# Moving the differences of the down weights from VectorE in a down projection to GpSimd in the mixers, with GpSimd's own loads and stores

## The chip, the cores and the metric

The kernel runs on one core of one Trainium2 chip. The metric is the time on the device in microseconds, from one launch. Engines are named as the profile names them: PE is TensorE (matmul), with PEld its weight loads; DVE is VectorE; ACT is ScalarE; POOL is GpSimd; SP is SyncE, which here only issues transfers. Each engine takes its instructions in order, its DMA issues among them. On-chip memory is SBUF, and PE writes to PSUM.

## The reference, cut to what matters

One layer of a hybrid encoder runs on a prompt of 2048 rows and on 128 sample rows, all of width 1024 in float32:

```python
h = rms_norm(x, norm_g[0])
z = h @ w_in                      # q, k, v of attention; q, k, v, o and two gates of the mLSTM
att = band_attention(qa, ka, va)  # chunks of 64, own chunk + 8 before, learned relative bias
hb = mlstm_sequence(qh, kh, vh, ig, lf, ...)
mix = concat(rms_norm(att), sigmoid(ob) * head_norm(hb)) @ w_out
x = x + rms_norm(mix, norm_g[1])
u = rms_norm(x, norm_g[2]) @ w_up                 # 1024 -> 2 x 2816
y = causal_depthwise_conv(u, width=3)
gate, up = split(y)
x = x + rms_norm((gelu(gate) * up) @ w_down, norm_g[3])     # w_down: 2816 x 1024
```

Matmuls are made accurate by splitting each operand into a high part `h` and a rest `l`, and three matmuls `hh + hl + lh` per product (`mm3`, L102 to L106).

## The kernel before, in words

**Mixers.** The prompt is worked in two halves of 8 tiles of 128 rows; the sample tile goes with the first. In each half, 14 groups of 256 columns of `w_in` are projected one after the other (`va0`, `qk0`, `qk1`, `va1`, `qk2`, `qk3`, then `qb` and `vo` in turn). A loop (L1245) walks the groups; each group is a generator that yields after every 12 matmuls. After each yield, `pump` (L183) lets two further streams go on, attention and mLSTM, by a balance of estimated PE and DVE times. PE makes `qk` in PSUM, ACT copies it out as `qk_st` (L236, L238) and issues its store to `qTd` or `kTd`; SP loads it again as `qraw` and `kraw`, and ACT and DVE split these into `qs`, `kh`, `kl`. `wi_h` and `wi_l` are the split weights of the next group. At the start `relrow` is built in device memory (the bias, one row per query), and its parts `nb` are loaded and edged on POOL (L338, L339). POOL also masks `mb` of the mLSTM (L685), makes the small roots `mf` from `ad` (L658, L659), and completes the keys `skr` of the sample attention (L860).

**Feed-forward.** The 17 tiles go in three blocks. Each block runs an up projection (22 steps), then a down projection. Blocks 1 and 2 multiply by a fast 2 x 2 scheme with 7 products in place of 8, which needs differences of the four blocks of 512 columns `B11, B12, B22, B21` in which `w_down` is laid out (11 rows of four blocks). Block 0's down projection takes the plain weights, 22 steps for each half of the columns (`dh` 0 and 1). Beside it, one row of four blocks in every four steps is loaded, turned into differences on DVE and stored in device memory as `wtd`, from where `down_rows` (L1363) loads it in blocks 1 and 2 under the name `wdr`. `gr` and `gh`, `gl` are the activations, `fr` the copy of a finished PSUM tile (L1394), `h2T_pt`, `b` and `t` the transposed input of the next block's up projection. At the switch from `dh` 0 to 1 six tiles are copied to `fr` by DVE, and PE's next matmuls write where they lay.

**Order.** The program text gives an order, and a scheduler places instructions on each engine by its own estimate of times. Instructions wrapped in `keep_in_program_order` keep their order among each other. Tiles come from pools with a fixed number of buffers; the four tiles of a row come from `spare`:

```python
spare = ctx.enter_context(tc.tile_pool(name="spare", bufs=6, reuse_waits="tile"))    # L56

for k in ks:                                   # down projection, block 0
    ...
    for j in order if k == NF - 1 else range(nt):
        down(j, k, wh, wl)
    if k >= 1:
        ahead.step()
    if b == 0:
        next(fold, None)                       # L1866
```

A row's third and fourth tile therefore wait until stores of the row before have landed. `store_a` (L1576) makes the matching differences of the activations in blocks 1 and 2 on DVE.

## Time and profile before

| | us |
|---|---|
| three runs, median (lowest to highest) | 2769.21 (2767.95 to 2771.8) |
| the profiled execution | 2768.76 |
| its span, first to last instruction | 2767.0 |
| PE, DVE, ACT, POOL busy | 2693.8, 1943.2, 1438.5, 654.3 |

Stretches by name: the first projections begin at 12 us, the mixers and `w_out` end near 1316 us, block 0's up projection runs to 1638 us, its down projection to 1840 us, and blocks 1 and 2 follow.

How to read it: a group row shows line, engine, operation, output and inputs, shape, count, then busy us, mean ns of one, and the idle us before with what ended them. A row in order of time starts with its start and duration in us; in brackets stands how long the engine was idle before, and what released it. A row of waits has us in total, times, longest. A matmul's end is modelled, so successive matmuls overlap in such rows. A row on an issue (`ACTq`, `SPq`, `POOLq`) has KB and the median us from issue to landing.

### The profile page before, as it was taken

What the parts mean: (1) busy time and instruction counts of PE and PEld (TensorE: products, weight loads), DVE (VectorE), ACT (ScalarE), POOL (GpSimd) and SP (SyncE); (2) the same over time, 40 slices, a digit from 0 to 9 for tenths busy, and PEclk for the clock granted to TensorE, in tenths of its full rate; (3) what the DMA queues carried; (4) which work ended last, traced back from release to release, by engine and by line L of the source; (5) the groups of instructions that cost most, each with busy time, mean ns of one, the idle gap of its engine ahead of it and who ended that gap; (6) DMA issues with size and microseconds to landing.
All of it is one profiled execution on the core that took longest, in us unless ns stands there. A gap on an engine that the chain in (4) does not pass through costs nothing.

```text
span 2767.0 us, 47747 instructions
## 1 busy us (share of the span) xinstructions
PE 2693.8 (97%) x16422; PEld 2520.4 (91%) x16422; DVE 1943.2 (70%) x3615; ACT 1438.5 (52%) x2918; POOL 654.3 (24%) x1271
## 2 busy tenths in 40 slices
PE   8999999999999999999999999999999999999998
PEld 7899999998899998878999998789999878999976
DVE  5344455646546668766989987668888876998956
ACT  4355555645356666543545455445455665554554
POOL 1000010211100002344434322123332212455401
PEclk9999999999999999999999999999999999999999
DMA  5534355556554456355645559866785777787775
GB/s 184 158 116 139 105 161 173 158 155 210 166 180 143 140 168 195 108 167 196 229 153 187 168 189 326 300 222 205 230 239 174 248 235 231 222 257 230 247 261 178
DMA packets 326017, 536.11 MB, mean 194 GB/s; under 512 B 60002, under 2 KB 159806, under 8 KB 325646
## 3 DMA queue, kind: packets, MB, share of 16 engines
q1 hardware_dynamic: 248382, 393.82, 45.7%
q0 software_dynamic: 32464, 93.87, 10.4%
q10 hardware_dynamic: 44928, 45.37, 5.1%
q8 instruction: 129, 2.11, 0.3%
q14 instruction: 114, 0.93, 0.1%
HBM read 383.28 MB, written 159.08 MB: 196 GB/s over the span
## 4 chain that ended last, share of the span: by engine, by line
PE 53%; DVE 3%; DMA 2%; issue 1%; POOL 1%; ACT 1%; DVEq 0%; POOLq 0%; SPq 0%; ACTq 0%
PE uec L104 6%; PE uec L105 6%; PE uec L106 6%; PE dn L106 4%; PE dn L105 4%; PE dn L104 4%; PE ua L106 3%; PE ua L105 3%; PE ua L104 3%; PE wo L106 2%; PE wo L104 2%; PE wo L105 2%; PE dnm L106 2%; PE dnm L105 2%; PE dnm L104 2%
## 5 line engine op out<-in xcount | busy, mean ns | idle before, releaser
L104 PE MATMUL uec<-B,wuh 128*128 128x384 f32 (+1 forms) x720 | 236.1, 328 | 4.1 <-DVE uu L1644 4.1
L105 PE MATMUL uec<-B,wuh 128*128 128x384 f32 (+1 forms) x720 | 235.3, 327 | 0.0
L106 PE MATMUL uec<-B,wul 128*128 128x384 f32 (+1 forms) x720 | 234.1, 327 | 0.0
L1309 ACT CAST wuh<-wu 128x512 fp32r<-128x512 f32 x255 | 141.7, 618 | 108.8 <-PE uec L105 100.9
L1310 DVE TENSOR_TENSOR wul<-wu,wuh 128x512 fp32r<-128x512 f32 x255 | 165.5, 685 | 4.0 <-DMA x2d<-mx 2.8
L405 DVE CUSTOM_DVE_ANT_0 tmp<-s,nb 128x640 f32<-128x640 f32 (+4 forms) x128 | 94.4, 737 | 95.1 <-PE s L395 93.5
L104 PE MATMUL vo<-wi_h,hT 128*128 128x256 f32 x544 | 155.1, 285 | 0.6 <-DVE mt L211 0.6
L106 PE MATMUL vo<-wi_h,hT 128*128 128x256 f32 x544 | 155.6, 286 | 0.0
L105 PE MATMUL vo<-wi_l,hT 128*128 128x256 f32 x544 | 154.8, 285 | 0.0
L104 PEld LDWEIGHTS uec<-B,wuh 128*128 128x128 f32 x720 | 135.2, 188 | 6.6 <-DVE uu L1644 5.5
L104 PE MATMUL qk<-hT,wi_h 128*128 128x384 f32 (+1 forms) x384 | 128.5, 335 | 7.3 <-ACT qk_st L236 5.9
L105 PEld LDWEIGHTS uec<-B,wuh 128*128 128x128 f32 x720 | 135.4, 188 | 0.3
L106 PEld LDWEIGHTS uec<-B,wul 128*128 128x128 f32 x720 | 135.1, 188 | 0.0
L418 DVE TENSOR_TENSOR ptl<-pt,pth 128x640 fp32r<-128x640 f32 (+4 forms) x128 | 93.6, 737 | 55.9 <-ACT pth L417 54.8
L406 ACT ACTIVATE tmp<-tmp,mn 128x640 f32<-128x640 f32 (+4 forms) x128 | 97.6, 762 | 67.0 <-DVE mn L405 62.9
L1310 DVE TENSOR_TENSOR wdl<-wdr,wdh 128x512 fp32r<-128x512 f32 x198 | 125.1, 685 | 7.3 <-ACT wdh L1309 7.0
L1310 DVE TENSOR_TENSOR al<-ar,ah 128x768 fp32r<-128x768 f32 (+2 forms) x94 | 70.9, 764 | 82.5 <-ACT ah L1309 81.0
L105 PE MATMUL qb<-hT,wi_h 128*128 128x384 f32 (+1 forms) x384 | 127.9, 333 | 0.0
L105 PE MATMUL qk<-hT,wi_h 128*128 128x384 f32 (+1 forms) x384 | 127.5, 332 | 0.0
L106 PE MATMUL qk<-hT,wi_l 128*128 128x384 f32 (+1 forms) x384 | 127.2, 331 | 0.0
L106 PE MATMUL qb<-hT,wi_l 128*128 128x384 f32 (+1 forms) x384 | 127.2, 331 | 0.0
L104 PE MATMUL qb<-hT,wi_h 128*128 128x384 f32 (+1 forms) x384 | 127.1, 331 | 0.0
(445 smaller groups left out, 9373.0 us busy)
## 6 DMA issues: line engine op xcount, KB each, us to landing
wu<-in_w_up SPq DMA_DIRECT2D x220, 256.0 KB, 4.9
wu<-wsd SPq DMA_DIRECT2D x176, 256.0 KB, 4.8
wdr<-in_w_down SPq DMA_DIRECT2D x110, 256.0 KB, 5.0
wi_raw<-in_w_in SPq DMA_DIRECT2D x52, 512.0 KB, 4.0
wsd<-ws POOLq DMA_DIRECT2D x88, 256.0 KB, 3.6
wdr<-wtd SPq DMA_DIRECT2D x88, 256.0 KB, 5.3
gr<-gd SPq DMA_DIRECT2D x39, 384.0 KB, 6.0
kraw<-kTd SPq DMA_DIRECT2D x112, 128.0 KB, 3.2
```

Of the source, the lines that this page charges most:

```text
L104: nc.tensor.matmul(out, ah, bh, start=start, stop=False, skip_group_check=onto)
L105: nc.tensor.matmul(out, ah, bl, start=False, stop=False, skip_group_check=onto)
L106: nc.tensor.matmul(out, al, bh, start=False, stop=stop, skip_group_check=onto)
L405: nc.vector.tensor_tensor_reduce(o_, s_, b_, 1.0, 3e38, ALU.add, ALU.min, accum_out=mn)
L406: nc.scalar.activation(tmp[:, :n], tmp[:, :n], AF.Exp, bias=mn, scale=-1.0, accum_out=rsum[:, i % 4, hh:hh + 1])
L418: nc.vector.tensor_tensor(s.ptl[:, sl, qc], ptv, s.pth[:, sl, qc], op=ALU.subtract)
L1309: nc.scalar.copy(h, r)
L1310: nc.vector.tensor_tensor(l, r, h, op=ALU.subtract)
```

## The change: what it does

The generator of the differences is started before the mixers and advanced once after each yield of the first half's projection groups, from group 1 (`qk0`) on, until its 99 steps are through, and no longer in block 0's down projection. Loads, subtractions and stores are all on POOL; before, they were on ACT's queue, DVE and POOL's queue. Loads and stores stay of 256 KB, and the number of each stays 44. The third difference is formed with the other sign, so the fourth is a sum, and `store_a` gives the matching activation difference the other sign too.

```diff
+FOLD_AT = 1
...
-    def folds(period, plan):
+    def folds():
+        keep = tc.keep_in_program_order
         live = {}
 
         def load(k, xs):
             if k < NK:
                 for x in xs:
                     live[k, x] = spare_tile(f"fold{k}_{x}")
-                    tc.keep_in_program_order(nc.scalar.dma_start(live[k, x], I["w_down"][k][:, x * 512:(x + 1) * 512]))
+                    keep(nc.gpsimd.dma_start(live[k, x], I["w_down"][k][:, x * 512:(x + 1) * 512]))
 
-        def combine(k):
+        def store(k, xs):
+            for x in xs:
+                keep(nc.gpsimd.dma_start(wtd[k][:, x * 512:(x + 1) * 512], live.pop((k, x))))
+
+        for k in range(NK):
+            load(k, (0, 1))
+            yield
+            load(k, (2, 3))
+            yield
+            yield
+            yield
             a, b, c, d = [live[k, x] for x in range(4)]
-            for o, x, y in ((a, b, a), (b, c, b), (c, c, a), (d, d, c)):
-                tc.keep_in_program_order(nc.vector.tensor_tensor(o, x, y, op=ALU.subtract))
-
-        def store(k):
-            if k >= 0:
-                for x in range(4):
-                    tc.keep_in_program_order(nc.gpsimd.dma_start(wtd[k][:, x * 512:(x + 1) * 512], live.pop((k, x))))
-        ...
+            for o, x, y, op in ((a, b, a, ALU.subtract), (b, c, b, ALU.subtract), (c, a, c, ALU.subtract),
+                                (d, d, c, ALU.add)):
+                keep(nc.gpsimd.tensor_tensor(o, x, y, op=op))
                 yield
-        if live:
-            store(NK - 1)
+            store(k, range(4))
+            yield
...
             pump(pe + sum(a[0] for a in ahead), dve + sum(a[1] for a in ahead))
+            if half == 0 and gi >= FOLD_AT:
+                next(fold, None)
...
-    fold = folds(4, {0: ("ab",), 1: ("cd",), 3: ("combine", "store")})
...
-            for o, x, y in ((s3, a11, a21), (s2, a22, s3), (s4, a12, s2)):
-                nc.vector.tensor_tensor(o, x, y, op=ALU.subtract)
+            for o, x, y, op in ((s3, a11, a21, ALU.subtract), (s2, s3, a22, ALU.subtract), (s4, a12, s2, ALU.add)):
+                nc.vector.tensor_tensor(o, x, y, op=op)
...
-                    if b == 0:
-                        next(fold, None)
```

Three places of the new order. POOL, early in the mixers, before: after the last norm of the first half it has only the edging of `nb` and the masks `mb`, in this row.

```order
L338 MEMSET nb_0_1243 64x64
L339 MEMSET nb_0_1243 64x64
L338 MEMSET nb_0_1314 64x64
L339 MEMSET nb_0_1314 64x64
L685 AFFINE_SELECT mb_0_4002<-mb_0_4002 128x256
L685 AFFINE_SELECT mb_2_4103<-mb_2_4103 128x256
```

POOL at the same place, now. The whole first row of blocks (loads, four operations, stores) and the second's loads stand ahead of this piece; `fold_0` to `fold_3` are the four blocks of a row.

```order
L1194 TENSOR_TENSOR fold_0_1110<-fold_1_1112,fold_0_1110 128x512
L1194 TENSOR_TENSOR fold_1_1112<-fold_2_1147,fold_1_1112 128x512
L1194 TENSOR_TENSOR fold_2_1147<-fold_0_1110,fold_2_1147 128x512
L1194 TENSOR_TENSOR fold_3_1149<-fold_3_1149,fold_2_1147 128x512
L339 MEMSET nb_0_1271 64x64
L340 MEMSET nb_0_1271 64x64
L1182 DMA wtd_244<-fold_0_1110 128x512
L1182 DMA wtd_244<-fold_1_1112 128x512
L1182 DMA wtd_244<-fold_2_1147 128x512
L1182 DMA wtd_244<-fold_3_1149 128x512
L1178 DMA fold_0_1313<-in_w_down 128x512
L1178 DMA fold_1_1315<-in_w_down 128x512
```

The small operations now stand between pieces of the work on the differences, and before the first `mb` three rows of blocks are done and the fourth is half loaded. Later on, the last two rows of blocks stand so among `skr` and `ad`:

```order
L861 COPY skr_0_3873<-own_3871 128x16
L1194 TENSOR_TENSOR fold_0_3780<-fold_1_3782,fold_0_3780 128x512
L861 COPY skr_1_3893<-own_3871 128x16
L861 COPY skr_2_3917<-own_3871 128x16
L1194 TENSOR_TENSOR fold_1_3782<-fold_2_3802,fold_1_3782 128x512
L1194 TENSOR_TENSOR fold_2_3802<-fold_0_3780,fold_2_3802 128x512
L861 COPY skr_3_3948<-own_3871 128x16
L1194 TENSOR_TENSOR fold_3_3804<-fold_3_3804,fold_2_3802 128x512
```

Behind this piece come four stores, four loads and one more subtraction, and only then `ad` and `mf`; before, the four `skr` and `ad` followed each other directly.

ACT at the first attention head, in the second group's projections, before (`kTd` and the like are stores, `qk` is PSUM):

```order
L236 COPY qk_0_st_0_1052<-qk_0_1_0_984 128x384
L251 DMA kTd_0_81<-qk_0_st_0_1052 128x384
L354 CAST qs_0_1274<-qraw_0_1247 128x512
L236 COPY qk_0_st_1_1094<-qk_0_1_1_1055 128x384
L251 DMA kTd_0_81<-qk_0_st_1_1094 128x128
L251 DMA kTd_1_82<-qk_0_st_1_1094 128x256
```

And now:

```order
L237 COPY qk_0_st_0_1064<-qk_0_1_0_994 128x384
L252 DMA kTd_0_81<-qk_0_st_0_1064 128x384
L237 COPY qk_0_st_1_1114<-qk_0_1_1_1067 128x384
L252 DMA kTd_0_81<-qk_0_st_1_1114 128x128
L252 DMA kTd_1_82<-qk_0_st_1_1114 128x256
L355 CAST qs_0_1306<-qraw_0_1275 128x512
```

The cast `qs`, which needs the load `qraw`, has moved behind one more copy out of `qk`. On PE, the matmuls of attention move back by some tens of projection matmuls in the same stretch, and from the place where the last difference is stored the two orders of PE are alike.

DVE at the switch of block 0's down projection, before:

```order
L1394 COPY fr_0_20510<-dn_0_1_19636 128x512
L1310 TENSOR_TENSOR gl_1_1_20573<-gr_1_1_20464,gh_1_1_20572 128x768
L1181 TENSOR_TENSOR fold_0_20456<-fold_1_20458,fold_0_20456 128x512
L1310 TENSOR_TENSOR wdl_1_20531<-wdr_1_0_20532,wdh_1_20530 128x512
L1181 TENSOR_TENSOR fold_1_20458<-fold_2_20488,fold_1_20458 128x512
L1310 TENSOR_TENSOR wdl_1_20531<-wdr_1_1_20536,wdh_1_20530 128x512
L1181 TENSOR_TENSOR fold_2_20488<-fold_2_20488,fold_0_20456 128x512
L1310 TENSOR_TENSOR wdl_1_20531<-wdr_1_2_20540,wdh_1_20530 128x512
L1133 TENSOR_TENSOR t_20756<-h2T_pt_1_0_20749,b_20721 128x512
L1394 COPY fr_0_20492<-dnm_0_0_19633 128x512
```

And now:

```order
L1400 COPY fr_0_20598<-dn_0_1_19812 128x512
L1316 TENSOR_TENSOR gl_1_1_20661<-gr_1_1_20556,gh_1_1_20660 128x768
L1316 TENSOR_TENSOR wdl_1_20619<-wdr_1_0_20620,wdh_1_20618 128x512
L1316 TENSOR_TENSOR wdl_1_20619<-wdr_1_1_20624,wdh_1_20618 128x512
L1316 TENSOR_TENSOR wdl_1_20619<-wdr_1_2_20628,wdh_1_20618 128x512
L1134 TENSOR_TENSOR t_20828<-h2T_pt_1_0_20821,b_20793 128x512
L1400 COPY fr_0_20580<-dnm_0_0_19809 128x512
```

The three subtractions between the splits of `wdr` are gone; the rest keeps its order.

More of the change, by code (lines that the diff above doesn't have):

```diff
@@ L1175, in load @@
                     live[k, x] = spare_tile(f"fold{k}_{x}")
-                    tc.keep_in_program_order(nc.scalar.dma_start(live[k, x], I["w_down"][k][:, x * 512:(x + 1) * 512]))
-        def combine(k):
-            a, b, c, d = [live[k, x] for x in range(4)]
-            for o, x, y in ((a, b, a), (b, c, b), (c, c, a), (d, d, c)):
-                tc.keep_in_program_order(nc.vector.tensor_tensor(o, x, y, op=ALU.subtract))
-        def store(k):
-            if k >= 0:
-                for x in range(4):
-                    tc.keep_in_program_order(nc.gpsimd.dma_start(wtd[k][:, x * 512:(x + 1) * 512], live.pop((k, x))))
-        acts = dict(ab=lambda k: load(k, (0, 1)), cd=lambda k: load(k, (2, 3)), combine=combine, store=store,
-                    before=lambda k: store(k - 1))
-        for k in range(NK):
-            for step in range(period):
-                for what in plan.get(step, ()):
-                    acts[what](k)
+                    keep(nc.gpsimd.dma_start(live[k, x], I["w_down"][k][:, x * 512:(x + 1) * 512]))
[9 more added lines that the diff above has]
+            yield
+            a, b, c, d = [live[k, x] for x in range(4)]
+            for o, x, y, op in ((a, b, a, ALU.subtract), (b, c, b, ALU.subtract), (c, a, c, ALU.subtract),
+                                (d, d, c, ALU.add)):
+                keep(nc.gpsimd.tensor_tensor(o, x, y, op=op))
                 yield
-        if live:
-            store(NK - 1)
+            store(k, range(4))
+            yield
     GROUPS = ["va0", "qk0", "qk1", "va1", "qk2", "qk3", "qb0", "vo0", "qb1", "vo1", "qb2", "vo2", "qb3", "vo3"]
@@ L1237, in hymba_step @@
     chunks = []
+    fold = folds()
     norms = norm_steps(0)
@@ L1300, in hymba_step @@
                 mems.append(lambda i=i: mlstm_sample(i))
+    for _ in fold:
+        pass
     for cost in out:
@@ L1883, in hymba_step @@
                     unfinished.append((tiles[j], rs))
-        if b == 0:
-            for _ in fold:
-                pass
         if not last:
```

## The prediction

> **What bounds the kernel now.** I read the page first, then the busy time by stretches, then what the matrix engine (PE) waits for, and last the order in time at the places where it waits.
>
> ```profile
> span 2767.0 us, 47747 instructions
> PE 2693.8 (97%) x16422; PEld 2520.4 (91%) x16422; DVE 1943.2 (70%) x3615; ACT 1438.5 (52%) x2918; POOL 654.3 (24%) x1271
> ```
>
> PE is busy for 2693.8 of 2767.0 us, so all its idle time together is 73.2 us. The change alters no matmul. It can only remove or add idle time of PE, and the question is how much of those 73 us lies where the change works. The stretches answer that: start, PE, PEld, DVE, ACT, POOL busy (with counts), then PE's clock, DMA share, GB/s.
>
> ```profile
> 40.00:75.00 35.00, 32.39 (x208) 30.74 (x207) 14.00 (x61) 8.91 (x20) 1.32 (x6) 1.00 0.47 155
> 75.00:115.00 40.00, 33.35 (x181) 31.66 (x181) 9.31 (x27) 11.21 (x28) 0.77 (x2) 0.96 0.54 148
> 115.00:400.00 285.00, 284.88 (x2034) 281.83 (x2033) 136.64 (x303) 145.16 (x336) 8.54 (x29) 1.00 0.42 127
> 1638.00:1840.00 202.00, 196.27 (x878) 159.71 (x877) 141.00 (x203) 95.93 (x164) 40.58 (x78) 1.00 0.85 290
> ```
>
> The last row is the down projection of block 0, where the differences are made now. PE idles there for 202.00 - 196.27 = 5.73 us, with DVE busy 70% and the DMA engines 85%. The first three rows are where the work goes: PE idles 2.61 us, then 6.65 us, then 0.12 us. From 115 to 400 us PE is full and DVE is under half busy. So the prize is at most 5.7 us, the long middle of the new home is cheap, and the risk sits at its beginning.
>
> **What leaves the down projection.**
>
> ```profile
> L1181 DVE TENSOR_TENSOR fold<-fold,fold 128x512 f32<-128x512 f32 x44 | 30.2, 686 | 1.9 <-DMA fold<-in_w_down 1.7
> fold<-in_w_down ACTq DMA_DIRECT2D x44, 256.0 KB, 5.7
> wtd<-fold POOLq DMA_DIRECT2D x44, 256.0 KB, 6.2
> PE dn L104 <- DVE fr L1394: 2.0, 2, 1.5
> PE h2T_pt L1107 <- ACT b L1124: 1.6, 1, 1.6
> PE dn L104 <- DVE ug L1484: 1.1, 2, 0.9
> PE h2T_pt L1107 <- DVE t L1133: 0.9, 1, 0.9
> ```
>
> 44 subtractions of 686 ns leave DVE (30.2 us of its 141.0 us), 44 loads leave ACT's queue and 44 stores POOL's: 88 x 0.262 MB = 23.1 MB of the 202 us x 290 GB/s = 58.6 MB that move there, 39%. Nearly all of those 30 us lie beside PE and buy nothing. The last four rows (us, times, longest) are all of PE's waits there, 5.6 us. All but the 1.1 us on `ug`, which precede the first subtraction, fall at the switch from the first half of the columns to the second. In order of time that place reads:
>
> ```profile
> 1740.25 1.29 DVE L1394 COPY fr<-dn 128x512 f32<-128x512 f32 x2 [2.56 <-PE dn L106]
> 1742.32 0.69 DVE L1181 TENSOR_TENSOR fold<-fold,fold 128x512 f32<-128x512 f32 x1
> 1743.75 0.69 DVE L1181 TENSOR_TENSOR fold<-fold,fold 128x512 f32<-128x512 f32 x1
> 1745.22 0.69 DVE L1310 TENSOR_TENSOR wdl<-wdr,wdh 128x512 fp32r<-128x512 f32 x1 [0.79 <-ACT wdh L1309]
> 1742.49 0.62 ACT L1309 CAST wdh<-wdr 128x512 fp32r<-128x512 f32 x1 [1.65 <-DMA wdr<-in_w_down]
> 1744.57 1.23 ACT L1309 CAST wdh<-wdr 128x512 fp32r<-128x512 f32 x2 [1.46 <-DMA wdr<-in_w_down]
> 1746.35 0.66 PE L1107 MATMUL h2T_pt<-ident,x2r 128*128 128x128 f32 x4 [1.64 <-ACT b L1124]
> ```
>
> The first gap stays: `fr` waits for PE's own last matmul and PE waits for `fr` (1.5 us of the 2.0). The other three (0.5, 1.6 and 0.9 us, 3.0 together) come from late work on ACT and DVE: ACT is held twice (1.65 and 1.46 us) by weight loads `wdr` that come late on crowded DMA engines, and DVE does four subtractions between the copies that PE needs. In the new order the subtractions are gone and 39% of the traffic with them. I take the whole 3.0 us as gained; the ends are 0 (the loads are late for another reason, the chain from `wdr` to `b` stands) and 5.7 us (all idle time goes). What is late next is the first `fr`. ACT's issuing of 44 loads is in none of PE's waits, so that it goes counts nothing.
>
> **What the mixers take on.** The trace has no subtraction of this shape on POOL. The nearest row is an addition of twice the width.
>
> ```profile
> L1039 POOL TENSOR_TENSOR mx<-mx 128x1024 f32<-128x1024 f32 x17 | 41.0, 2410 | 2.5 <-DVE mx L1038 2.5
> L1186 POOL DMA_DIRECT2D wtd<-fold x44 | 24.2, 550 | 104.2 <-DVE fold L1181 102.3 <-issue 1.6
> ```
>
> Half of 2410 is 1205 ns, so 44 of them are about 53 us, and 88 DMA issues of 550 ns are 48 us: some 101 us on an engine that is busy 1.32 + 0.77 + 8.54 = 10.6 us between 40 and 400 us. A row of blocks needs loads (5.7), four operations (4.8), four issues (2.2) and, for two of the six buffers, the landing of a store (6.2), about 19 us, and eleven rows about 208 us. They fit into the stretch up to 400 us, so POOL's own time costs nothing. Three things can reach PE.
>
> First, the order on POOL. The small operations that others wait for now stand behind subtractions and behind DMAs that land 5.7 to 6.2 us later. The last rows of blocks meet the sample attention and the first memory heads:
>
> ```profile
> 361.52 1.35 POOL L860 COPY skr<-own 128x16 f32<-128x16 f32 x3 [9.75 <-ACT wi_h L1219]
> 379.69 0.19 POOL L658 TENSOR_SCALAR ad<-ad 128x2 f32<-128x2 f32 x1 [15.12 <-DVE ad L656]
> ```
>
> By the new order three subtractions slip in among these copies (3.6 us late), then four stores, four loads, the landing of both and one subtraction precede `ad` at 379.69: 4 x 0.55 + 6.2 + 2 x 0.55 + 5.7 + 1.2 = 16.4 us, against the 15.12 us that POOL waits there now. It comes out about 1 us late, in a stretch where PE has had no wait. I take +0.5 us; ends 0 and +4 (copies and `ad` both reach PE).
>
> Second, the DMA engines. The program order starts the loads at the first projection after the value group, when only POOL's own order holds them back, so they start when its last operation before them (`n_rs`) is done, near 43 us. Rows of blocks 0 to 2 and half of the loads of row 3 (26 transfers, 6.8 MB) fall before the first `mb` at 111 us, on top of 35 x 155 + 40 x 148 GB/s = 11.3 MB.
>
> ```profile
> 42.90 0.55 POOL L93 TENSOR_TENSOR n_rs<-n_ms,nhalf 128x1 f32<-128x1 f32 x1
> 111.62 0.77 POOL L685 TENSOR_SCALAR_AFFINE_SELECT mb<-mb 128x256 f32<-128x256 f32 x2 [39.59 <-DMA mb<-md]
> 65.00:75.00 10.00, 10.00 (x61) 9.14 (x60) 4.34 (x24) 1.77 (x5) 0.58 (x4) 1.00 0.93 306
> 75.00:85.00 10.00, 7.38 (x42) 6.74 (x42) 3.13 (x10) 2.51 (x5) 0.00 (x0) 1.00 0.36 73
> 100.00:110.00 10.00, 6.74 (x36) 6.42 (x36) 0.00 (x0) 0.64 (x2) 0.00 (x0) 0.92 0.89 256
> 81.46 0.62 ACT L354 CAST qs<-qraw 128x512 fp32r<-128x512 f32 x1 [10.29 <-DMA qraw<-qTd]
> 81.99 0.47 ACT L236 COPY qk_st<-qk 128x384 f32<-128x384 f32 x1
> 108.26 0.48 ACT L236 COPY qk_st<-qk 128x384 f32<-128x384 f32 x1 [8.10 <-DMA qraw<-qTd]
> PE qk L104 <- ACT qk_st L236: 5.9, 2, 3.3
> ```
>
> The bias rows of the attention are written out here, and the engines are at 93% just before the stall at 82 us and at 89% during that at 108 us. ACT stands for 10.29 and 8.10 us, and PE, which needs ACT to empty `qk`, idles for 5.9 us in two waits. More traffic lengthens both. Against that, the new order of ACT puts one more copy out of `qk` ahead of `qs`, and that is one 384-column group of about 4.2 us of matmuls (8 x 3 matmuls of 0.176 us, by 7.38 us of busy PE for 42 of them in the row of 75 us) that PE can run on. The two are of like size. I take 0, between -6 (both waits vanish) and +10 (see the slow rival).
>
> Third, the port between POOL and DVE, priced by the only places where POOL does wide arithmetic beside DVE:
>
> ```profile
> 1272.63 2.39 POOL L1039 TENSOR_TENSOR mx<-mx 128x1024 f32<-128x1024 f32 x1
> 1272.69 3.40 DVE L1099 SCALAR_TENSOR_TENSOR x2r<-x2r,n_rs,g 128x1024 f32<-128x1024 f32 x1 [0.71 <-POOL n_rs L93]
> L1099 DVE SCALAR_TENSOR_TENSOR x2r<-x2r,n_rs,g x17: 1277/1285/3400, 1211.1 to 2264.6; 128x1024 f32<-128x1024 f32 x17
> 1322.11 0.69 DVE L1310 TENSOR_TENSOR wu<-ws,wu 128x512 fp32r<-128x512 f32 x1
> 1322.56 2.51 POOL L1039 TENSOR_TENSOR mx<-mx 128x1024 f32<-128x1024 f32 x1
> 1322.72 0.55 DVE L1621 TENSOR_TENSOR x<-x,ub 128x384 f32<-128x384 f32 x1
> 1323.18 2.44 DVE L1310 TENSOR_TENSOR wu<-ws,wu 128x512 fp32r<-128x512 f32 x1
> ```
>
> A DVE operation with two inputs in SBUF that begins during POOL's 2.39 us takes 3.40 instead of 1.285 us: it ran only when POOL was through. At 1323 us a split of 0.69 us takes 2.44. The addition `x<-x,ub` with one input from PSUM is not touched (0.55). The Trainium skill says so in "SBUF — State Buffer", "Who interferes with whom": with two SBUF inputs, DVE and a GpSimd instruction that reads SBUF shut each other out for a whole instruction. The trace agrees, with 3.40 against 1.285 us; by that rule this change would do best to leave the differences where they were. In the kernel each new operation can hold DVE for up to 1.2 us, 53 us in all, and DVE is 48% busy from 115 to 400 us. I take +0.5 us at PE; ends 0 and +5, a tenth of the 53.
>
> **Rest.** The sign changes in `store_a` exchange operands and a subtraction for an addition, same shapes: 0. Block 1 reads `wtd` only in its own down projection, in either kernel after the last store.
>
> **The sum.** -3.0 + 0.5 + 0 + 0.5 = -2.0 us. The profiled execution took 2768.76 us, 1.76 more than its span, and the median of the three runs, 2767.95 to 2771.8, is 2769.21, 0.45 above it. So 2768.76 - 2.0 = 2766.8 in that execution, and 2767.2 about the median. Differences under 0.2%, 5.5 us, are what a measurement of this kernel can about tell from no change.
>
> **Rivals.** *Slower: the start of the attention.* Place: ACT's `qs` and `qk_st` between 65 and 115 us. If a third of the 6.8 MB comes in the crowded 20 us (306 and 256 GB/s), the loads that ACT waits for land 2.3 MB / 0.3 MB per us, some 8 us, later, plus 2 us for `nb` and `mb` standing behind POOL's DMA waits: +10, so 2767.2 + 10 = 2777. It decides from +7.5 us on. For it: 93% and 89%, and ACT stands in order, so nothing slips by. Against: from 75 to 85 us the engines are at 36%, and the reordering. Chance 0.27. "DMA: Bandwidth & Descriptors" of the Trainium skill ("Issuing engines are not separate DMA queues") supports it: another issuing engine saves issue time only, since all share 16 engines. No run here shows the two side by side yet.
>
> *Slower: the locked port,* at its end of +5 instead of +0.5, by the row of 3.40 us: 2771.7, which is still within 0.2%. It needs another 3 us from `nb` or `mb` to pass the bound. Chance 0.11, half of it slower by over 0.2%.
>
> *Faster: the reordered start.* ACT's order alone removes both waits on `qk_st`: -6 more, 2761. For it: each stall is shorter (at most 3.3 us) than the 4.2 us that one more group gives. Against: the added traffic. Chance 0.18.
>
> *Nothing moves:* the waits at the switch hang on `wdr` alone and stay, the term is 0: 2770.2. Chance 0.12, within 0.2%.
>
> **Numbers.** My forecast, -2.0 give or take 3.5 us, has the other 0.32, of which 0.07 lies beyond -5.5 us. Faster by over 0.2%: 0.18 + 0.07 = 0.25. Slower: 0.27 + 0.055 = 0.33, rounded. Within: 0.42. Cases of both signs hold most of it; the likeliest one's own range is 2763 to 2771. The range for 8 in 10 runs from 2759, a little past the fast rival, to 2779, past the slow one, and leaves out its upper end (port and start together).
>
> **What would show it.** Right: the waits of PE in block 0's down projection fall from 5.6 to about 2.6 us and only `fr` and `ug` remain; the DMA share there falls from 0.85 to about 0.55; POOL's subtractions last about 1.2 us; PE stays full from 115 to 400 us. Wrong: PE idle between 40 and 115 us well above or below 9.3 us, POOL operations much longer than 1.2 us, or DVE splits of 0.69 us that take 1.9 with PE waiting behind them. If `wdr` still lands late at the switch, the first term falls.

## The result and the profile after

| | before | after |
|---|---|---|
| median of 6 runs each, side by side (lowest to highest), us | 2768.58 (2764.97 to 2771.8) | 2794.32 (2789.64 to 2800.97) |
| the profiled execution, us | 2768.76 | 2789.64 |
| its span, us | 2767.0 | 2787.9 |

The change makes the kernel slower: the ratio is 1.0087, 95% interval 1.0072 to 1.0102, or 24 us of 2768.58 (20 to 28 us). The two profiled executions lie 20.9 us apart, and the readings below explain that pair.

The head of the page after:

```profile
span 2787.9 us, 47694 instructions
PE 2699.6 (97%) x16422; PEld 2523.8 (91%) x16422; DVE 1930.5 (69%) x3571; ACT 1437.0 (52%) x2918; POOL 733.7 (26%) x1359
```

PE has the same 16422 matmuls. It is busy 5.8 us longer (2699.6 against 2693.8) and idle 88.3 us instead of 73.2, 15.1 more; the two make the 20.9 us. The stretches say where (start, length, PE, PEld, DVE, ACT, POOL busy, PE's clock, DMA share, GB/s). After first, then the row of before for 400 to 450 us, which the prediction did not show:

```profile
40.00:75.00 35.00, 31.18 (x198) 29.32 (x197) 14.37 (x61) 8.71 (x20) 19.25 (x27) 1.00 0.70 221
75.00:115.00 40.00, 33.66 (x176) 32.63 (x175) 10.03 (x22) 9.26 (x20) 15.18 (x24) 0.91 0.92 240
115.00:400.00 285.00, 273.38 (x1939) 270.64 (x1938) 138.09 (x282) 136.19 (x316) 73.43 (x102) 0.98 0.56 172
400.00:450.00 50.00, 46.21 (x309) 42.14 (x308) 27.88 (x70) 24.08 (x65) 12.74 (x28) 1.00 0.65 201
1656.00:1858.00 202.00, 196.58 (x883) 160.34 (x882) 114.49 (x159) 95.60 (x161) 15.86 (x33) 1.00 0.55 177
```

```profile
400.00:450.00 50.00, 48.65 (x365) 46.74 (x364) 30.95 (x86) 27.07 (x75) 4.48 (x17) 1.00 0.66 193
```

Busy time alone misleads in these rows, since PE is busy for longer with the same matmul when its clock is lower (a 128x384 matmul 0.34 us before the wait at 311.74 us, 0.52 behind it). The start, 40 to 115 us, has only 0.9 us less of busy PE (64.84 against 65.74), but 15 matmuls fewer (374 and 389, added over the two rows), at a clock of 0.91 instead of 0.96 in its second row. So the matmuls are counted here, in the order in which PE starts them in each of the two traces. The 400th starts 0.2 us later than in before, the 700th (at 127.43 us in before) 6.1 us later, the 1700th (271.13) 6.2, the 2500th (378.44) 11.4 and the 2900th (436.22) 23.4 us later. From there to the 14000th the lag stays between 21 and 24 us. The loss thus lies in three places: 6 us at the start of the attention, 5 us near 300 us, and 12 us between 378 and 436 us. (The kernel without differences, shown below, has the order of before in the mixers and in its one trace also starts the 700th matmul 2.5 us late, but loses nothing in the other two places; so a part of the 6 us can be chance.) Between the first two nothing is lost, before and after:

```profile
135.00:270.00 135.00, 135.00 (x929) 134.16 (x928) 65.63 (x135) 68.93 (x153) 0.98 (x7) 1.00 0.42 125
135.00:270.00 135.00, 135.00 (x927) 134.18 (x927) 66.84 (x135) 68.26 (x155) 27.29 (x41) 1.00 0.55 167
```

POOL does some 26 us of the new work there, and PE stays full. The order of PE's matmuls differs between the kernels in the first two places, but from the 2422nd on all but five stand alike as far as the down projection, so the last 12 us are not due to PE's order.

The down projection of block 0 idles 5.42 instead of 5.73 us, with its DMA share down from 0.85 to 0.55 and DVE's work down by 26 us: the relief came, and it bought 0.3 us.

PE's waits between 40 and 450 us in after (us in total, times, longest):

```profile
PE pt L77 <- ACT tmp L407: 5.9, 4, 2.3
PE spt L77 <- ACT stmp L893: 4.8, 1, 4.8
PE mp L77 <- DVE mrow L576: 4.3, 1, 4.3
PE ss L105 <- ACT skh L865: 2.0, 1, 2.0
PE qk L105 <- ACT qk_st L239: 2.0, 1, 2.0
```

The wait that the prediction watched, for `qk_st`, fell from 5.9 to 2.0 us. In its place stand waits for attention (`tmp`, the exponentials of the prompt; `stmp`, `skh`, of the sample rows) and, once, for the mLSTM's `mrow`. In order of time, one row of the start and then the two longest waits of the middle read so (start, duration, then in brackets the idle time before and its releaser):

```profile
87.16 0.62 ACT L355 CAST qs<-qraw 128x512 fp32r<-128x512 f32 x1 [8.76 <-DMA qraw<-qTd]
309.57 4.64 POOL L1194 TENSOR_TENSOR fold<-fold,fold 128x512 f32<-128x512 f32 x3 [0.45 <-DMA fold<-in_w_down]
310.05 1.14 ACT L1220 CAST wi_h<-wi_raw 128x512 fp32r<-128x512 f32 x2 [5.52 <-DMA wi_raw<-in_w_in]
310.70 2.37 DVE L1221 TENSOR_TENSOR wi_l<-wi_raw,wi_h 128x512 fp32r<-128x512 f32 x2 [5.59 <-ACT wi_h L1220]
311.74 0.69 PE L77 MATMUL pt<-ident,tmp 128*128 128x128 f32 x2 [2.27 <-ACT tmp L407]
384.91 0.54 POOL L1178 DMA_DIRECT2D fold<-in_w_down  x1 [0.93 <-DMA wtd<-fold]
391.82 0.62 ACT L914 CAST svh<-svr 128x512 fp32r<-128x512 f32 x1 [7.47 <-DMA svr<-in_cache_v]
392.48 1.80 POOL L1194 TENSOR_TENSOR fold<-fold,fold 128x512 f32<-128x512 f32 x1 [7.04 <-DMA fold<-in_w_down]
395.31 0.73 ACT L893 ACTIVATE stmp<-stmp,smn 128x528 f32<-128x528 f32 x1 [2.57 <-DVE smn L889]
396.19 1.33 PE L77 MATMUL spt<-ident,stmp 128*128 128x128 f32 x5 [4.79 <-ACT stmp L893]
```

Read upward from PE. At 89.48 us PE has waited 4.3 us for `mrow`, which DVE makes behind its part of `qs`; ACT had stood 8.76 us for `qraw`, the load that the prediction's slow rival names. At 311.74 PE waits 2.27 us for `tmp`, which ACT could not make: ACT stood 5.52 us for the next group's weights `wi_raw`. The two splits that follow on DVE take 2.37 us where two of 0.69 take 1.38, under three subtractions that POOL does in the same time. At 396.19 PE waits 4.79 us for `stmp`; ACT had stood 7.47 us for the sample values `svr` while POOL's next load, issued at 384.91, was just as late (7.04 us).

The DMA share and the clock around both places:

```profile
300.00:305.00 5.00, 5.00 (x34) 5.00 (x33) 1.32 (x7) 1.61 (x5) 1.07 (x2) 1.00 0.96 294
310.00:315.00 5.00, 3.26 (x11) 3.26 (x12) 3.27 (x5) 2.97 (x8) 4.84 (x5) 0.67 0.26 74
385.00:390.00 5.00, 5.00 (x37) 5.00 (x36) 0.00 (x0) 0.00 (x0) 0.45 (x1) 1.00 0.88 269
395.00:400.00 5.00, 3.81 (x17) 3.73 (x18) 2.89 (x14) 2.94 (x9) 0.92 (x2) 0.50 0.26 82
```

The DMA engines are at 0.96 and 0.88 of full in slices shortly before the two waits, although the stretch of 285 us has a mean of 0.56. At both places the granted clock falls, to 0.67 and 0.50 of a 5 us slice; in slices of 1 us it is halved from 312 and from 394 us on, some 2 us after PE's last matmul. Not every wait brings that: in before, PE waits 2.62 us until 82.51 us, and the clock stays at 1.00. Between 40 and 450 us PE is busy for 14.4 us at the halved clock in after and for 3.0 us in before, which is worth some 5.7 us (an estimate: half of the difference). That explains most of PE's longer busy time in the mixers, but not the 5.8 us of the whole pair: before has such spells behind 450 us, for 13.2 us of its busy time against 3.1 in after, so that the mean clocks of the two executions are nearly the same, 0.996 and 0.995.

### The profile page after: what moved, and what is told of

It is laid out like the page before. It is cut to its first block, busy times and chain, and to the rows that moved or that the text cites. A ratio compares the mean times of both kernels' runs of the same rounds, so it can differ in the third digit from the quotient of the medians.

```text
span 2787.9 us, 47694 instructions
## 1 busy us (share of the span) xinstructions
PE 2699.6 (97%) x16422; PEld 2523.8 (91%) x16422; DVE 1930.5 (69%) x3571; ACT 1437.0 (52%) x2918; POOL 733.7 (26%) x1359
## 4 chain that ended last, share of the span: by engine, by line
PE 52%; DVE 3%; DMA 2%; issue 1%; ACT 1%; POOL 1%; SPq 0%; DVEq 0%; POOLq 0%; ACTq 0%
PE uec L105 6%; PE uec L106 6%; PE uec L107 6%; PE dn L107 4%; PE dn L106 4%; PE dn L105 4%; PE ua L107 3%; PE ua L106 3%; PE ua L105 3%; PE wo L107 2%; PE wo L105 2%; PE wo L106 2%; PE dnm L107 2%; PE dnm L106 2%; PE dnm L105 2%; PE ub L105 1%
```

## The experiments

Times are medians; each set was timed beside the kernel before, which had medians of 2770.0 to 2770.6 us. Three questions: does leaving the down projection gain anything; is the loss in the mixers the subtractions' or the transfers'; and is it place, engine or queue.

**What the old place gives back.** The generator does nothing, and blocks 1 and 2 read the raw weights, as they do in all runs below that leave out a part of the differences:

```diff
-        for k in range(NK):
-            load(k, (0, 1))
...
+        return
+        yield
...
-            src = I["w_down"][k] if blk < 4 else wtd[k]
+            src = I["w_down"][k]
```

> Left out: the differences of the down weights altogether; nothing is loaded, subtracted or stored for them, and blocks 1 and 2 load the plain blocks in their place. This is the floor that both kernels share. All theories: the idle time of PE in block 0's down projection falls by the 2 to 3 us that the change also gained there, and nothing is added to the mixers, so 2765 to 2767 us against 2769 of the kernel before and 2794 of the changed one.

Measured 2771.35 us, ratio 1.0003 (0.999 to 1.0017): no change that can be measured, where 2765 to 2767 us were expected. PE's waits in its down projection:

```profile
PE dn L105 <- DVE fr L1388: 1.5, 1, 1.5
PE dn L105 <- DVE ug L1477: 1.1, 2, 0.9
PE h2T_pt L1108 <- ACT b L1125: 0.7, 1, 0.7
PE h2T_pt L1108 <- DVE t L1134: 0.7, 1, 0.7
PE dnm L105 <- ACT gh L1303: 0.4, 1, 0.4
```

With no differences anywhere these waits are 4.4 us instead of 5.6. Of the 3.0 us that were forecast to go (0.5 of `fr`, 1.6 of `b`, 0.9 of `t`), 1.6 went and 0.4 came new with `gh`; in after `b` has 1.7 us, although the DMA share is 0.55. The rest of the wait at the switch is not due to the differences. By the lower end of the interval the change could win at most some 3 us (0.1%), wherever it put them.

**The subtractions alone.** 44 subtractions on POOL on four tiles filled once, no loads, no stores:

```diff
+        for x in range(4):
+            live[x] = spare_tile(f"fold_{x}")
+            keep(nc.gpsimd.memset(live[x], 0.0))
...
-            a, b, c, d = [live[k, x] for x in range(4)]
+            a, b, c, d = [live[x] for x in range(4)]
```

> Left out: the loads and stores of the differences. The 44 subtractions on GpSimd stay in the mixers, on four tiles that are filled once. Theory of traffic (the transfers delay loads that ACT waits for): 2766 to 2769, like e1_none. Theory of the port (GpSimd's subtractions shut DVE out): some 20 us over e1_none, 2785 to 2790. Theory of the queue (small operations stand behind GpSimd's waits on transfers): close to e1_none, at most 3 us over it.

Measured 2780.37 us, ratio 1.0031 (1.0014 to 1.0049): 9 us above the kernel without differences, in which PE does all matmuls in the same order. The two intervals just touch, so the size is rough, and it lies in none of the three ranges expected.

**The transfers alone.** The 44 loads and 44 stores on POOL's queue, no subtractions:

```diff
-            for o, x, y, op in ((a, b, a, ALU.subtract), ...):
-                keep(nc.gpsimd.tensor_tensor(o, x, y, op=op))
+            for _ in range(4):
                 yield
```

> Left out: the 44 subtractions. Loads and stores of 256 KB stay in the mixers on GpSimd's queue, blocks 1 and 2 load the plain blocks. Theory of traffic: most of the loss stays, 2783 to 2792. Theory of the port: like e1_none, 2765 to 2769. Theory of the queue: most of the loss stays, as with traffic; e6_thin tells the two apart.

Measured 2786.16 us, ratio 1.005 (1.0033 to 1.0067): 15 us above the kernel without differences. The two parts, 9 and 15, add up to the 24 us; with such intervals that is no proof that they simply add.

**Bytes or issues.** The same with 16 of each 512 columns:

```diff
-                    keep(nc.gpsimd.dma_start(live[k, x], I["w_down"][k][:, x * 512:(x + 1) * 512]))
+                    keep(nc.gpsimd.dma_start(live[k, x][:, :16], I["w_down"][k][:, x * 512:x * 512 + 16]))
```

> Like e3_dma_only, but each of the 88 transfers moves 16 columns of 512, so 0.72 MB in place of 23.1 MB; number, places and waits of GpSimd's issues stay. Theory of traffic: the loss goes, 2765 to 2770. Theory of the queue, and theory that the scheduler's other order of PE and ACT is what costs: the loss stays, 2780 or more.

Measured 2774.25 us, ratio 1.0013 (1.0002 to 1.0024): between the two ranges expected, but most of the 15 us is gone. And with 256 of each 512 columns, in a later set:

```diff
+                    keep(nc.gpsimd.dma_start(live[k, x][:, :256], I["w_down"][k][:, x * 512:x * 512 + 256]))
```

> Loads and stores alone, as in the kernel that took 2786.2 us, but of 256 of each 512 columns: half of the bytes in as many transfers; no subtractions, block 0's T matrices are read from the weights as they came. Theory A (the bytes fill the DMA engines when ScalarE's next loads are due): between the 2774.3 of 16 columns and the 2786.2 of all, 2776 to 2781, with fewer waits of ScalarE for loads between 300 and 430 us. Theory D (the order that the scheduler makes of the program around long transfers, not the traffic): 2784 to 2788 where the order is that of the whole transfers, about 2774 where it is that of the short ones, and not between.

Measured 2778.19 us, ratio 1.0024 (1.0011 to 1.0038), between the two, as theory A had it. The groups of ACT's casts between 115 and 450 us show the path (count, then busy, mean ns, then idle before and what ended it). In before:

```profile
L1219 ACT CAST wi_h<-wi_raw 128x512 fp32r<-128x512 f32 x40 | 22.9, 620 | 15.8 <-DMA wi_raw<-in_w_in 10.1 <-DMA vobd<-vo_st 2.2 <-PE qk L105 1.6
L367 ACT CAST vhl<-vraw 128x256 fp32r<-128x256 f32 x13 | 5.2, 401 | 8.3 <-DMA vraw<-vd 8.3
```

In the kernel without differences:

```profile
L1208 ACT CAST wi_h<-wi_raw 128x512 fp32r<-128x512 f32 x40 | 22.8, 620 | 17.5 <-DMA wi_raw<-in_w_in 13.8 <-PE qk L106 1.6 <-DMA qTd<-qk_st 1.2
L368 ACT CAST vhl<-vraw 128x256 fp32r<-128x256 f32 x13 | 5.2, 402 | 8.3 <-DMA vraw<-vd 8.3
```

With 16 columns:

```profile
L1217 ACT CAST wi_h<-wi_raw 128x512 fp32r<-128x512 f32 x38 | 21.7, 620 | 18.4 <-DMA wi_raw<-in_w_in 14.8 <-PE qk L106 2.7 <-PE qb L106 0.9
L368 ACT CAST vhl<-vraw 128x256 fp32r<-128x256 f32 x13 | 5.2, 402 | 7.2 <-DMA vraw<-vd 7.2
```

With 256 columns:

```profile
L1217 ACT CAST wi_h<-wi_raw 128x512 fp32r<-128x512 f32 x38 | 21.7, 620 | 19.0 <-DMA wi_raw<-in_w_in 17.0 <-PE qk L106 1.6 <-PE qb L106 0.4
L368 ACT CAST vhl<-vraw 128x256 fp32r<-128x256 f32 x13 | 5.2, 402 | 8.9 <-DMA vraw<-vd 8.8
```

With all columns, no subtractions:

```profile
L1217 ACT CAST wi_h<-wi_raw 128x512 fp32r<-128x512 f32 x36 | 20.5, 619 | 25.8 <-DMA wi_raw<-in_w_in 20.8 <-PE qb L106 3.2 <-DMA qTd<-qk_st 1.1
L368 ACT CAST vhl<-vraw 128x256 fp32r<-128x256 f32 x13 | 5.2, 403 | 19.7 <-DMA vraw<-vd 19.7
```

And in after:

```profile
L1220 ACT CAST wi_h<-wi_raw 128x512 fp32r<-128x512 f32 x36 | 20.5, 618 | 24.8 <-DMA wi_raw<-in_w_in 22.5 <-PE qk L106 2.3
L368 ACT CAST vhl<-vraw 128x256 fp32r<-128x256 f32 x12 | 4.8, 403 | 16.1 <-DMA vraw<-vd 16.1
```

ACT's wait for these two loads together is 18.4 us in before and 22.1 without differences; with transfers it goes 22.0, 25.8, 40.5 us as the bytes grow, and after has 38.6. The issues alone cost little: 16 columns are 3 us above no transfers. One reservation: the scheduler counts the transfers in its estimates. PE's order is the same with no differences and with 16 columns, and 93 of its 16422 places differ between 16 and 256 columns, but 930 between 256 columns and all. So a part of the last 8 us, from half to whole transfers, can be order; and the intervals of the 4 us before overlap.

**Port or occupied POOL.** Fills have no input, so they take POOL's time without its reading anything beside DVE. Three fills for each subtraction take about as long:

```diff
-                keep(nc.gpsimd.tensor_tensor(o, x, y, op=op))
+                for n in (512, 512, 256):
+                    keep(nc.gpsimd.memset(o[:, :n], 0.0))
```

> Left out: the differences; in the place of each subtraction on GpSimd stand three fills (512, 512 and 256 columns, some 1.36 us together), which take GpSimd's time but read nothing from SBUF. e2_sub_only cost 9 us over e1_none (2780.4 against 2771.4). Theory of the port (DVE's two-input operations wait while GpSimd reads SBUF): the 9 us go, 2769 to 2773. Theory of the queue (GpSimd's small operations come late behind the long ones): they stay, 2777 to 2783.

Measured 2776.52 us, ratio 1.0014 (1.0002 to 1.0026). That is below the subtractions' 2780.37, just under the range of the theory of the queue and well above that of the port, but the intervals overlap, so both were doubled. Every subtraction twice:

```diff
+                for _ in range(2):
+                    keep(nc.gpsimd.tensor_tensor(o, x, y, op=op))
```

> Every one of the 44 subtractions is done twice, 88 of 1.3 us in the mixers, with no loads and stores, and block 0's T matrices are read from the weights as they came (so this part of the output is not the reference's). The 44 alone took 2780.4 us, 9 us above the kernel without differences. Theory A (the subtractions hold up VectorE's work by the memory that both engines use): the cost doubles, 2787 to 2792 us, and the mean of VectorE's 128x512 splits goes from 766 ns to about 840. Theory B (the 9 us are chance between executions, or one order that fell badly): within 4 us of 2780.

Six fills for each:

```diff
+                    for n in (512, 512, 256) * 2:
+                        keep(nc.gpsimd.memset(o[:, :n], 0.0))
```

> Six fills in place of each subtraction, some 100 us of work on GpSimd in the mixers that reads nothing, where three gave 2776.5 us; no loads and stores, block 0's T matrices are read from the weights as they came. Theory A (the shared way into memory): the splits on VectorE keep 688 ns, as with three fills, and the time stays below that of 88 subtractions by 5 us or more, 2774 to 2782. Theory C (GpSimd's small operations come late behind the new work, whatever it is): as slow as the 88 subtractions, 2787 to 2792, with idle time of TensorE behind VectorE's or ScalarE's work that waited for skr, mf, mb.

Measured 2790.63 us, ratio 1.0067 (1.0044 to 1.009), for the subtractions, and 2781.69 us, ratio 1.0042 (1.0028 to 1.0056), for the fills. DVE's splits of `wi_raw` between 40 and 450 us, first with no differences:

```profile
L1209 DVE TENSOR_TENSOR wi_l<-wi_raw,wi_h 128x512 fp32r<-128x512 f32 x48 | 31.3, 688 | 30.7 <-ACT wi_h L1208 29.9 <-PE pt L77 0.7
```

With 44 subtractions:

```profile
L1221 DVE TENSOR_TENSOR wi_l<-wi_raw,wi_h 128x512 fp32r<-128x512 f32 x46 | 33.6, 766 | 27.7 <-ACT wi_h L1220 27.7
```

With 88 subtractions:

```profile
L1222 DVE TENSOR_TENSOR wi_l<-wi_raw,wi_h 128x512 fp32r<-128x512 f32 x44 | 37.3, 883 | 19.8 <-ACT wi_h L1221 19.8
```

With the doubled fills:

```profile
L1221 DVE TENSOR_TENSOR wi_l<-wi_raw,wi_h 128x512 fp32r<-128x512 f32 x44 | 28.7, 688 | 28.5 <-ACT wi_h L1220 28.4
```

And in after:

```profile
L1221 DVE TENSOR_TENSOR wi_l<-wi_raw,wi_h 128x512 fp32r<-128x512 f32 x44 | 34.0, 800 | 40.2 <-ACT wi_h L1220 40.1
```

The mean goes 688, 766, 883 ns with the subtractions, is 800 in after, and stays 688 with the fills: POOL's subtractions hold DVE's splits up, and its fills do not. The time points the same way, by 9 us between the doubled kernels. The fills are not free either (5 us above the kernel without differences, and 10 doubled). Theory A would therefore explain about half of the subtractions' 9 us. What the other half is, POOL's small operations coming late or an order that falls worse, stays open: the kernels with fills and the doubled ones differ in order as well, 24 of the 132 fills (48 of the 264) run before 40 us, where the first subtraction begins at 45.2, and the intervals of the doubled pair still overlap.

**Traffic without tiles.** 88 copies of 256 KB inside device memory, issued by POOL, with nothing that waits for them but POOL's own next issues (11 times, 12.1 us in all for the half of them that goes to `wtd`):

```diff
+                    keep(nc.gpsimd.dma_start((wtd if n < 8 else ghost)[k][:, x * 512:(x + 1) * 512],
+                                             I["w_down"][k][:, x * 512:(x + 1) * 512]))
```

> Left out: the differences. In the mixers, at the same places, GpSimd issues 88 copies of 256 KB from device memory to device memory, with no tile and no wait of GpSimd on them but for the few slots of its queue. Theory of traffic: as slow as e3_dma_only or slower, 2783 to 2795. Theory that GpSimd's waits on loads and stores cost: like e6_thin, 2772 to 2776.

Measured 2819.02 us, ratio 1.0162 (1.0137 to 1.0188), 48 us above the kernel without differences. That is far beyond the 2783 to 2795 expected, and the run does not compare directly: a copy reads and writes device memory, where a load or a store does one of the two, and no buffer holds it back. The first is issued at 2.1 us, where after has its first load at 43.5, and PE's 300th matmul, at 54 us in before, already starts 17.5 us late. The other 30 us arise behind it; the DMA share from 75 to 115 us is 0.95. Traffic alone, without any engine's work on it, can thus cost TensorE tens of microseconds, but more than a third of them here lies ahead of the place of the change.

**Place alone.** The change with the subtractions on DVE and the loads on ACT's queue, as they were before, but in the mixers:

```diff
-                    keep(nc.gpsimd.dma_start(live[k, x], ...))
+                    keep(nc.scalar.dma_start(live[k, x], ...))
...
-                keep(nc.gpsimd.tensor_tensor(o, x, y, op=op))
+                keep(nc.vector.tensor_tensor(o, x, y, op=op))
```

> The changed kernel with the subtractions back on DVE and the loads back on ACT's queue; only the place is new. Theory of traffic: the 12 to 15 us of the transfers stay, and the 9 us of GpSimd's subtractions go, 2782 to 2788. Theory that GpSimd is at fault for all of it: 2769 to 2773.

Measured 2780.01 us, ratio 1.0028 (1.0016 to 1.004), just under the 2782 to 2788 of the theory of traffic. Place alone costs 9 us of the 24, and the engine and the queue the rest. It carries all the transfers and yet costs less than the transfers on POOL's queue without any subtraction; ACT issues the loads between its own casts, so that they can't run ahead of it. That reading was not tested apart from the order.

**Engine alone.** The kernel before with its 44 subtractions on POOL, still in the down projection:

```diff
-                tc.keep_in_program_order(nc.vector.tensor_tensor(o, x, y, op=ALU.subtract))
+                tc.keep_in_program_order(nc.gpsimd.tensor_tensor(o, x, y, op=ALU.subtract))
```

> The kernel before with the 44 subtractions on GpSimd at their old place, block 0's down projection, loads on ACT's queue as before. My prediction's first term (30 us less on DVE there buys little): 2768 to 2772, no measurable difference. Theory of the port: the splits there have two inputs in SBUF and can be held 44 times for up to 1.3 us, and PE is fed by them: 2773 to 2778.

Measured 2783.06 us, ratio 1.0047 (1.0033 to 1.0061), 12.5 us slower for 30 us less work on DVE, and above both ranges expected. Two groups of splits between 1640 and 1850 us, in before:

```profile
L1310 DVE TENSOR_TENSOR wdl<-wdr,wdh 128x512 fp32r<-128x512 f32 x42 | 26.9, 685 | 2.7 <-ACT wdh L1309 2.6
L1310 DVE TENSOR_TENSOR gl<-gr,gh 128x768 fp32r<-128x768 f32 (+1 forms) x47 | 41.4, 887 | 47.1 <-ACT gh L1309 34.7 <-DMA gr<-gd 12.3
```

With the subtractions on POOL:

```profile
L1310 DVE TENSOR_TENSOR wdl<-wdr,wdh 128x512 fp32r<-128x512 f32 x44 | 44.3, 1058 | 1.4 <-ACT wdh L1309 1.3
L1310 DVE TENSOR_TENSOR gl<-gr,gh 128x768 fp32r<-128x768 f32 (+1 forms) x47 | 50.9, 1096 | 47.7 <-ACT gh L1309 46.8 <-DMA wdr<-in_w_down 0.9
```

685 became 1058 ns and 887 (a mean of two shapes) became 1096: 44 x 373 + 47 x 209 ns = 26 us of DVE's time, nearly as much as the 30 us that the move took off it. PE now waits five times, 2.5 us in all, for `gl`, which is among none of its waits in before.

**A later place.** The change with its generator advanced in the second half, from the seventh group on:

```diff
-FOLD_AT = 1
+FOLD_AT = 6
...
-            if half == 0 and gi >= FOLD_AT:
+            if half == 1 and gi >= FOLD_AT:
```

> The change as it is, but the differences made in the second half of the projections, from its seventh group on, where GpSimd and the DMA engines are less busy than in the first half. Theory A (cost by what the transfers and subtractions meet): the transfers meet no burst of loads for the attention, so that 5 to 15 us of the 24 are saved, 2778 to 2788. Rival (any place in the mixers costs the same, since TensorE is full in all of them): 2791 to 2796. A gain below 2768 is not expected by either, since the kernel without any differences took 2771.4.

Measured 2811.39 us, ratio 1.0147 (1.0123 to 1.017). Both expectations missed: it costs 41 us. So its two parts were run alone there, by the edits shown above for each: the transfers, and then the subtractions.

> Loads and stores alone, in the second half of the projections from its seventh group on, where the whole change took 2811.4 us; no subtractions, block 0's T matrices are read from the weights as they came. Theory A (ScalarE's waits for loads make the cost there too): most of the 41 us, 2792 to 2805. Rival (the subtractions collide with the attention's longer work on VectorE, which is denser there): 2772 to 2785.

> The 44 subtractions alone at that late place, no loads and stores, block 0's T matrices are read from the weights as they came. Theory A: about what they cost in the first half, 2776 to 2785. Rival (the subtractions are what costs there): 2790 to 2805.

Measured 2804.21 us, ratio 1.0119 (1.0091 to 1.0146), and 2785.92 us, ratio 1.005 (1.003 to 1.0069). The transfers make most of it: 33 us above the kernel without differences, against 15 in the first half, and the subtractions 15 against 9 (0.9 us above the range expected). The stretch from 700 to 1070 us in before:

```profile
700.00:1070.00 370.00, 362.83 (x2680) 351.51 (x2679) 224.57 (x526) 217.53 (x519) 26.68 (x83) 1.00 0.54 163
```

With the transfers alone at the later place:

```profile
700.00:1070.00 370.00, 348.71 (x2530) 337.99 (x2528) 201.23 (x468) 195.06 (x459) 69.64 (x158) 0.98 0.68 208
```

A mean share of 0.54 looked like room. But ACT is busy for 59% of this stretch in before, against 51% of that from 115 to 400 us (145.16 of 285), and PE idles 7.2 us in it already, against 0.12: a late load would find less slack there, though no run tests that by itself. With the transfers PE is busy for 14.1 us less, and it starts 150 matmuls fewer, some 21 us at the pace of before (an estimate from the two counts).

**Half the pace.** The change advanced at every second unit, from the same group on, into the second half:

```diff
-            if half == 0 and gi >= FOLD_AT:
+            if half * 14 + gi >= FOLD_AT and u % 2 == 0:
```

> The change as it is, but one step of it at every second unit of the projections, from the first half's second group into the second half: the same transfers and subtractions over twice the time. Theory A (queues form where a burst of transfers meets a burst of the attention's loads): fewer meet at once, 2780 to 2790. Rival (each transfer and each subtraction costs its own amount wherever it stands): 2790 to 2800.

Measured 2796.12 us, ratio 1.009 (1.007 to 1.0109), as slow as the change itself. That is the rival's range, but not its reason: the same transfers and subtractions cost 41 us at the later place, so they don't cost the same wherever they stand. And the trace shows that the half pace loses little where the change loses its first 11 us:

```profile
115.00:400.00 285.00, 282.14 (x2013) 278.85 (x2011) 138.24 (x299) 142.92 (x333) 42.21 (x71) 1.00 0.49 151
```

PE starts 2013 matmuls there, against 2034 in before and 1939 in after. Its 2500th matmul starts 1.0 us later than in before (11.4 in after), with 21 of the 44 subtractions begun by 400 us, and ACT's wait for `wi_raw` and `vraw` up to 450 us is 22.0 us, as without differences. The loss comes behind that: 7.5 us at the 2900th matmul, 17.9 at the 4500th (662 us in before); the last store is issued at 679 us. In this one trace spreading the work took most of the loss out of the first place, and the stretch from 380 us on, into which it moved the rest, took the gain back. No run has the one without the other, so what spreading is worth stays open.

No version of those run is faster than the kernel before, and by the kernel without differences, 2771.35 us, there was at most some 3 us to be found this way.

## Why the prediction was wrong, step by step

The forecast was -2.0 us and the result about +24, beyond the slow rivals too.

**What leaves the down projection, -3.0.** The DMA share fell to the 0.55 named, and the wait for `fr` stayed, as said. But PE's idle time there fell by 0.3 us, and its waits by 1.2 with no differences at all. The step that failed is taking the whole of the waits at the switch for a consequence of the late `wdr` and of DVE's subtractions. The value was the end that the text gave, 0. The rival "nothing moves" was right about this term, and only about this one.

**The DMA engines, 0 with ends -6 and +10.** This is the step that failed most, by about 15 us. The mechanism of the rival at the start of the attention is the one that acted: ACT stands in order, and a late load on a crowded set of DMA engines holds everything behind it. But the prediction looked for it only between 65 and 115 us, because PE waits there in before, and set it off against the reordering. The reordering did come (`qk_st` 5.9 to 2.0 us), but the waits for `mrow` and `tmp` took its place and the clock fell, so that the start cost up to 6 us of the profiled pair, subtractions included, and not 0. The sign named for it, PE's idle time between 40 and 115 us, hardly moved (10.2 us against 9.3), since a part of the loss is slower matmuls and a part stands behind 115 us. The other 17 us arose where PE had been full. The trace of before shows ACT's waits for loads there too (18.4 us for `wi_raw` and `vraw`), just short enough that PE had matmuls to go on with. The transfers brought them to about 40 us, past that slack. Reading only where PE waits, and the mean share of 0.42, hid that.

The Trainium skill's "DMA: Bandwidth & Descriptors", section "Issuing engines are not separate DMA queues", holds that transfers issued by any engine run on the same 16 DMA engines and interleave. The runs agree: loads of SP (`wi_raw`, `vraw`, `svr`) landed late beside transfers of POOL's queue, more so with more bytes.

**The port, +0.5 with ends 0 and +5.** The lock was real (766, 800 and 883 ns in place of 688), its size too small: the subtractions cost 9 us, of which the lock is perhaps half. The text put 0.5 us at PE, and for the end a tenth of 53 us, by no row. In the down projection, where DVE is denser, the engine alone costs 12.5 us.

**POOL's order, +0.5.** POOL's own time and issues fit, as worked out: a subtraction has a median of 1292 ns (1205 was the estimate), and the last store is issued at 415 us where about 400 was said. (A row of blocks has eight issues, not the four of the sum; it does not matter, since the rows keep the pace of the loop that advances them, from 43.5 to 415 us in place of the 208 us that the sum gave.)

```profile
L1194 POOL TENSOR_TENSOR fold<-fold,fold x44: 1266/1292/1835, 48.6 to 411.1; 128x512 f32<-128x512 f32 x44
L1182 POOL DMA_DIRECT2D wtd<-fold x44: 539/542/636, 53.9 to 415.2; - x44
```

None of PE's five longest waits is for a POOL operation, but the fills, which take POOL's time and leave DVE's splits at 688 ns, cost 5 us, so the 0.5 may have been too small as well.

**The clock.** No term stood for it. The estimate above puts it at some 5.7 us in the mixers of the profiled pair, a quarter of the loss there. "TensorE: Matmul & The Clock Gate" of the Trainium skill, section "HAM oscillation — how this bites in real kernels", says that an idle gap over about 3.4 us brings the clock down. The trace agrees that the clock falls, in the gap of 4.79 us (to 0.50), but it fell sooner: some 2 us into that gap, and also after one of 2.27 us (0.67).

## What to carry to other kernels

On an engine that never waits, ask how near its feeders are to making it wait: read their waits for loads in the stretch where it is full, since that slack is what new traffic spends. A mean DMA share of 0.5 is no room when every load is needed just in time: a transfer moved there costs what its burst delays, which here ranged from nothing (135 to 270 us) to 12 us within 60 us. To find where a loss arises, count how far an engine has come in its own order; its busy time in a fixed stretch hid most of the first loss here. Before moving work out of a stage, take it out altogether: if that gains nothing, a new place can hardly gain more.

## What had not been expected of the hardware

A subtraction of 128x512 on POOL costs DVE nearly what it saves it: 26 us of longer splits for 30 us of work moved off it in the down projection. Fills on POOL leave DVE's splits at 688 ns. A PE idle for 2.27 us was granted 0.67 of its clock over the 5 us around it, while one idle for 2.62 us kept its full clock. A wait can thus cost more than its length: between 40 and 450 us of the profiled pair 14.9 us more idle time, and some 5.7 us of slower matmuls.
